# A hybrid decoder step: 64-token states in place of a 128-token product level, and the heads' tails split over two TensorE visits

## The chip, the core and the metric

The kernel runs on one core of a Trainium2 chip. The metric is the device time of one execution in microseconds (us); lower is better. The kernel before takes 1199.65 us (median of 3 runs, 1199.41 to 1201.19). Differences of 0.2% (2.4 us) are about what a measurement can tell here.

## What is computed

Two layers over a prompt group (16 learned meta tokens and 256 prompt tokens) and a sample group (8 sequences of 8 tokens), 336 columns in all. Layer 0 is a gated linear recurrence (HGRN2) with 16 heads of 128 x 128 state; layer 1 is sliding-window attention. The change touches layer 0 alone:

```python
def hgrn_chunk(q, logf, k, v, s0):
    b = jnp.cumsum(logf, axis=1)
    diff = jnp.where(causal, b[:, :, None] - b[:, None, :], -jnp.inf)
    a = jnp.sum(q[:, :, None] * jnp.exp(diff) * k[:, None, :], axis=-1)
    o = einsum('bthk,bhkv->bthv', q * exp(b), s0) + einsum('btsh,bshv->bthv', a, v)
    s_new = exp(b_last)[..., None] * s0 + einsum('bshk,bshv->bhkv', k * exp(b_last[:, None] - b), v)
    return o, s_new
# h = x @ w_in, split in q, fx, i, g; f = lb + (1-lb)*sigmoid(fx); k = 1-f; v = i
# prompt: a chunk of 16, then four of 64, the state handed on; sample: 8 tokens on a given state
# o * rsqrt(mean(o*o) + eps) * norm_w * silu(g), then o @ w_out, residual and LayerNorm
```

## The kernel before

All projections run as three fp32r matmuls (high and low halves of x and of the weights) into one PSUM tile `pj` per 128 output columns, issued by `Stream.run`. A head of layer 0 has four such tiles in the order f, q, i, g: 192 matmuls of 336 columns, two of whose operands wait for weights that ScalarE (ACT) and VectorE (DVE) split into `whi` and `wlo` seven chunks (of four times three matmuls) ahead. One call of `Stream.step` follows every three matmuls, and this "tick" is the clock of all side work: generators are spawned, and each `yield n` puts off the rest by n ticks. The order of the instructions on every engine is thus written out when the kernel is built; at run time an engine waits only where its next instruction's operands are late.

The recurrence of a head is `head_chain`. It doubles blocks: 1, 2, 4, 8, 16, 32, 64 tokens, `update` scaling k and q at each level by the running products `total`. TensorE is visited first for the levels 1 to 8 (tile `lv_a`, 48 products of 32 x 32), then for the levels 16, 32, 64 and 128 (tile `lv_b`, with the products `kr` x `qp` of 145 and 17 columns as the level of 128), then the transposes of k and v (`pk`, `pv`). ScalarE and VectorE gather all scores of a head in `at` and copy V, K, Vs, Ks out of PSUM; GpSimd (POOL) spreads Vs over `vm`.

What follows, `head_tail`, is a generator that the next head's chain advances (`adv(h - 1)`): outputs `po` and the prompt's last state `psp`; then squares and the norm (`ss`, raised to -1/2 on POOL); the scaled output `osc`; its transposes `pt` and the sample states' products `pss`; the gated output `og`, its halves `oh`, `ol`, and the sample states, scaled in place in `s0` and sent out. So TensorE is visited three times per head: `lv_a` with po and psp of the head before; pt and pss of the head before; `lv_b` with pk and pv. After the last head `tail_alone` advances the tail. PSUM has 3 tiles for `pj`, 2 for the levels (`lv`) and 3 for everything else (`mm`, taken by `pm`). The output projection (`z`, `oh` x `w_out`) follows head 15 at once; its first three tiles run chunk by chunk together.

Of the kernel before, what the change touches and what calls it, by code (L numbers as in the profile page):

```python
# [226 lines left out]
def hybrid_trunk(tc, x_prompt, x_sample, state_hgrn, cache_k, cache_v, meta, w_in0, lb_logits, norm_w, w_out0,  # L227
# [7 lines left out]
    with es:  # L235
# [84 lines left out]
        for nm, w in (("f", 384), ("qp", 448), ("iT", 384), ("ks", 256), ("at", 3 * 272), ("a32", 96), ("sq0", 256),  # L320
                      ("sq1", 256), ("w64", 64)):
            one[nm] = hp1.tile([P, w], F32, tag=nm, name=nm)
            nc.gpsimd.memset(one[nm], 1.0 if nm == "w64" else 0.0)
# [79 lines left out]
        def head_state(h):  # L403
            if h not in hd:
                hd[h] = dict(one, sq=one[f"sq{h % 2}"])
            return hd[h]

        def epi_f(h):
            def epi(ps):
# [11 lines left out]
                s0 = hp.tile([P, 8, P], F32, tag="s0", name=f"s0_{h}")  # L421
                nc.sync.dma_start(s0, state_hgrn[0, :, h].rearrange("b k v -> k b v"))
                d["s0"] = s0
# [8 lines left out]

        stage_of = {}
# [18 lines left out]
        def epi_g(h):  # L452
            def epi(ps):
                d = head_state(h)
                sg = hp.tile([P, T], F32, tag="sg", name=f"sg{h}")
                nc.scalar.activation(sg, ps, AF.Sigmoid)
                d["sg"] = sg

                def chain():
# [35 lines left out]

        tails = {}

        def adv(h):
            if h in tails:
                stage_of[h] += 1  # L500
                next(tails[h], None)

        def tail_alone(h):
            for w in (5, 4, 4, 2, 1):
                adv(h)
                yield w

        def head_chain(h):
            d = head_state(h)
            stage_of[h] = 0  # L510
            kr, qp, a32, s0, sq = d["kr"], d["qp"], d["a32"], d["s0"], d["sq"]
# [53 lines left out]
            adv(h - 1)  # L565
            yield 1
# [18 lines left out]
            nc.vector.tensor_tensor(t128[:, 1:2], t128[:, 0:1], t16, op=ALU.mult)  # L585
            nc.vector.tensor_scalar(qp[:, 255:272], qq[1][:, 255:272], t128[:, 0:1], None, op0=ALU.mult)
# [8 lines left out]
            yield 2  # L595
            adv(h - 1)
            yield 3
# [3 lines left out]
            pb = lv.tile([P, 512], F32, tag="lv", name=f"lv{h}_b")  # L601
            level(pb, 0, 4, wide=False)
            for blk in range(2):
# [5 lines left out]
                for a in range(2):  # L609
# [4 lines left out]
            nc.tensor.matmul(pb[:, 306:451], kr[:, 0:128], qp[:, 127:272], start=True, stop=True,  # L614
                             skip_group_check=True)
            nc.tensor.matmul(pb[:, 288:305], kr[:, 128:256], qq[1][:, 255:272], start=True, stop=True,
                             skip_group_check=True)
            iT = d["iT"]
            pk = pm(f"pk{h}")
            for j in range(2):  # L620
                nc.tensor.transpose(pk[:, j * P:(j + 1) * P], ks[:, j * P:(j + 1) * P], ident)
# [8 lines left out]
            for a in range(2):  # L630
                nc.scalar.copy(at[64 * a:64 * a + 32, 0:2, 64 * a + 31:64 * a + 63],
                               pb[64 * a:64 * a + 32, 96:160].rearrange("p (b w) -> p b w", b=2))
            nc.scalar.copy(at[0:64, 0:2, 63:127], pb[0:64, 160:288].rearrange("p (b w) -> p b w", b=2))
            for blk in range(3):
                nc.vector.copy_predicated(
                    at[:, blk, 0:128].rearrange("p (j w) -> p j w", w=32),
                    mk[:, 480 + blk * 128:608 + blk * 128].rearrange("p (j w) -> p j w", w=32),
                    a32[:, blk * 32:blk * 32 + 32].unsqueeze(1).to_broadcast([P, 4, 32]))
            nc.scalar.copy(at[:, 1, 127:144], pb[:, 288:305])
            nc.scalar.copy(at[:, 0, 127:272], pb[:, 306:451])  # L640
            V = hp.tile([P, 3, P], F32, tag="V", name=f"V{h}")
            K = hp.tile([P, 2, P], F32, tag="K", name=f"K{h}")
# [14 lines left out]
            tails[h] = head_tail(h, at, V, K, Ks, vm, fs)  # L657
            if h == H - 1:
                yield 6
                yield from tail_alone(h)  # L660

        def head_tail(h, at, V, K, Ks, vm, fs):
            d = head_state(h)
            s0, sq = d["s0"], d["sq"]
            po = pm(f"po{h}")
            psp = pm(f"psp{h}")
            for s in range(2):
                for j in range(4):
# [3 lines left out]
            nc.tensor.matmul(po[0:16, 256:384], at[:, 0, 256:272], V[:, 0, :], start=False, stop=False,  # L672
                             skip_group_check=True, tile_position=(0, 0))
            nc.tensor.matmul(po[0:16, 256:384], at[:, 1, 128:144], V[:, 1, :], start=False, stop=False,
                             skip_group_check=True, tile_position=(0, 0))
            nc.tensor.matmul(po[:, 256:384], at[:, 2, 0:128], V[:, 2, :], start=False, stop=True,
                             skip_group_check=True)
            nc.tensor.matmul(po[:, 128:256], at[:, 0, 128:256], V[:, 0, :], start=True, stop=False,
                             skip_group_check=True)
            nc.tensor.matmul(po[:, 128:256], at[:, 1, 0:128], V[:, 1, :], start=False, stop=True,  # L680
                             skip_group_check=True)
            nc.tensor.matmul(po[:, 0:128], at[:, 0, 0:128], V[:, 0, :], start=True, stop=True, skip_group_check=True)
            nc.tensor.matmul(psp[:, 0:128], K[:, 0, :], V[:, 0, :], start=True, stop=False)
            nc.tensor.matmul(psp[:, 0:128], K[:, 1, :], V[:, 1, :], start=False, stop=False)
            nc.tensor.matmul(psp[:, 0:128], K2, V[:, 2, :], start=False, stop=True)
            yield
            nc.gpsimd.tensor_tensor(s0, s0, fs.unsqueeze(2).to_broadcast([P, 8, P]), op=ALU.mult)
            sp = hp1.tile([P, P], F32, tag="sp", name=f"sp{h}")
            nc.scalar.copy(sp, psp[:, 0:128])
            nc.sync.dma_start(st_p[0, 0, h], sp)  # L690
# [11 lines left out]
            pt = pm(f"pt{h}")  # L702
            for j in range(3):
                nc.tensor.transpose(pt[:, j * P:(j + 1) * P], osc[:, j, :], ident)
            pss = []
            for u in range(2):
                pss.append(pm(f"pss{h}_{u}"))
                nc.tensor.matmul(pss[u], Ks[:, u, :], vm[0:112, 4 * u:4 * u + 4, :].rearrange("p b v -> p (b v)"),
                                 start=True, stop=True)
# [3 lines left out]
            nc.vector.scalar_tensor_tensor(og[:, 0:288], pt[:, 0:288], nw[:, h:h + 1], sg[:, 0:288], op0=ALU.mult,  # L713
                                           op1=ALU.mult)
# [5 lines left out]
            for u in range(2):  # L720
                s0u = s0[:, 4 * u:4 * u + 4, :].rearrange("p b v -> p (b v)")
                nc.vector.tensor_tensor(s0u, s0u, pss[u], op=ALU.add)
            nc.sync.dma_start(st_s[0, :, h].rearrange("b k v -> k b v"), s0)
# [641 lines left out]
```

## Time and profile before

| what | us |
|---|---|
| median of the runs | 1199.65 |
| the profiled execution | 1203.74 |
| its span | 1201.9 |
| TensorE busy in it | 1181.7 |
| VectorE busy | 793.3 |
| ScalarE busy | 625.6 |
| GpSimd busy | 244.0 |

Matmuls are pipelined and their ends are modelled, so what an instruction costs TensorE is read from its start to the next start. A fp32 product is two matmul instructions in the trace (x2 for one product).

### The profile page before, as it was taken

How to read it: one execution, taken by the hardware profiler on the slowest of the kernel's cores; microseconds unless marked ns; L12 is line 12 of the kernel's file. 1: busy time of each engine (PE TensorE's matmuls, PEld its weight loads, DVE VectorE, ACT ScalarE, POOL GpSimd, SP SyncE). 2: the span in 40 equal slices, each digit the busy share in tenths (PEclk: the TensorE clock that was granted, in tenths of full speed). 3: DMA queues.
4: the chain of work that ended last, by engine and by line, in shares of the span. 5: the costliest groups of instructions: out<-in, count | busy, mean ns of one | idle time of the engine just before them, and what ended most of it. 6: DMA issues, size and time to landing. Idle time of an engine off the chain costs nothing. (4 is left out here: it accounts for less than half of the span.)

```text
span 1201.9 us, 26362 instructions
## 1 busy us (share of the span) xinstructions
PE 1181.7 (98%) x10131; PEld 1135.6 (94%) x10131; DVE 793.3 (66%) x2017; ACT 625.6 (52%) x1827; POOL 244.0 (20%) x349
## 2 busy tenths in 40 slices
PE   9999999999999999999999999999999999999995
PEld 7999999999999999999999999988888899998994
DVE  4765666555666555656558777678778767776675
ACT  4655555554555454545445446665656655553330
POOL 3022112222112122112134332000000112144420
PEclk9999999999999999999999999999999999999997
DMA  9545654455654555654555555634244345564532
GB/s 263 157 134 150 178 144 133 137 144 157 178 144 120 150 144 159 167 149 119 150 144 140 145 146 165 182 105 129 73 117 127 90 123 159 152 170 139 148 89 88
DMA packets 328462, 171.48 MB, mean 143 GB/s; under 512 B 19084, under 2 KB 325612, under 8 KB 328166
## 3 DMA queue, kind: packets, MB, share of 16 engines
q1 hardware_dynamic: 327792, 168.82, 50.3%
q8 instruction: 80, 1.31, 0.5%
q0 software_dynamic: 544, 0.97, 0.2%
q14 instruction: 46, 0.38, 0.1%
HBM read 156.97 MB, written 14.42 MB: 143 GB/s over the span
## 5 line engine op out<-in xcount | busy, mean ns | idle before, releaser
L212 PE MATMUL pj_q<-xh,wlo_q 128*128 128x336 f32 (+1 forms) x512 | 165.9, 324 | 0.0
L212 PE MATMUL pj_g<-xh,wlo_g 128*128 128x336 f32 (+1 forms) x512 | 162.9, 318 | 0.0
L213 PE MATMUL pj_g<-xl,whi_g 128*128 128x336 f32 (+1 forms) x512 | 160.6, 314 | 0.0
L214 PE MATMUL pj_g<-xh,whi_g 128*128 128x336 f32 (+1 forms) x512 | 160.6, 314 | 0.0
L213 PE MATMUL pj_q<-xl,whi_q 128*128 128x336 f32 (+1 forms) x512 | 160.5, 314 | 0.0
L214 PE MATMUL pj_q<-xh,whi_q 128*128 128x336 f32 (+1 forms) x512 | 160.3, 313 | 0.0
L212 PEld LDWEIGHTS pj_q<-xh,wlo_q 128*128 128x128 f32 x512 | 96.7, 189 | 5.8 <-issue 4.7
L212 PEld LDWEIGHTS pj_g<-xh,wlo_g 128*128 128x128 f32 x512 | 96.7, 189 | 2.2 <-issue 1.3
L213 PEld LDWEIGHTS pj_g<-xl,whi_g 128*128 128x128 f32 x512 | 96.8, 189 | 0.8
L213 PEld LDWEIGHTS pj_q<-xl,whi_q 128*128 128x128 f32 x512 | 96.7, 189 | 0.5
L214 PEld LDWEIGHTS pj_g<-xh,whi_g 128*128 128x128 f32 x512 | 96.5, 189 | 0.0
L214 PEld LDWEIGHTS pj_q<-xh,whi_q 128*128 128x128 f32 x512 | 96.5, 189 | 0.0
L169 DVE TENSOR_TENSOR wlo_g<-raw_g,whi_g 128x512 fp32r<-128x512 f32 x128 | 90.4, 743 | 0.6 <-ACT whi_g L158 0.6
L169 DVE TENSOR_TENSOR wlo_q<-raw_q,whi_q 128x512 fp32r<-128x512 f32 x128 | 86.2, 684 | 3.9 <-ACT whi_q L158 3.9
L212 PE MATMUL pj_f<-xh,wlo_f 128*128 128x336 f32 x256 | 83.6, 326 | 0.0
L213 PE MATMUL pj_f<-xl,whi_f 128*128 128x336 f32 x256 | 81.5, 318 | 0.0
L212 PE MATMUL pj_i<-xh,wlo_i 128*128 128x336 f32 x256 | 81.4, 318 | 0.0
L214 PE MATMUL pj_f<-xh,whi_f 128*128 128x336 f32 x256 | 81.4, 318 | 0.0
L214 PE MATMUL pj_z<-oh,whi_z 128*128 128x336 f32 x256 | 81.1, 317 | 0.0
L212 PE MATMUL pj_z<-oh,wlo_z 128*128 128x336 f32 x256 | 81.1, 317 | 0.0
L213 PE MATMUL pj_z<-ol,whi_z 128*128 128x336 f32 x256 | 81.0, 316 | 0.0
L212 PE MATMUL pj_y<-ph,wlo_y 128*128 128x320 f32 x256 | 81.0, 316 | 0.0
(410 smaller groups left out, 3219.4 us busy)
## 6 DMA issues: line engine op xcount, KB each, us to landing
raw_g<-in_hgrn_w_in_dram SPq DMA_DIRECT2D x32, 512.0 KB
raw_z<-in_hgrn_w_out_dram SPq DMA_DIRECT2D x32, 512.0 KB
raw_q<-in_swa_w_in_dram SPq DMA_DIRECT2D x32, 512.0 KB
raw_g<-in_swa_w_in_dram SPq DMA_DIRECT2D x32, 512.0 KB
raw_y<-in_swa_w_out_dram SPq DMA_DIRECT2D x32, 512.0 KB
raw_f<-in_hgrn_w_in_dram SPq DMA_DIRECT2D x30, 512.0 KB
raw_q<-in_hgrn_w_in_dram SPq DMA_DIRECT2D x30, 512.0 KB
raw_i<-in_hgrn_w_in_dram SPq DMA_DIRECT2D x30, 512.0 KB
```

Source lines behind the costliest of these rows:

```text
L169: e.nc.vector.tensor_tensor(lo, t.pop(("raw", kc)), hi.bitcast(F32), op=ALU.subtract)
L212: nc.tensor.matmul(ps, lo[:, kk, :], xh, start=first, stop=False)
L213: nc.tensor.matmul(ps, hi[:, kk, :], xl, start=False, stop=False)
L214: nc.tensor.matmul(ps, hi[:, kk, :], xh, start=False, stop=last)
```

## The change

- The level of 128 is gone: no products of 145 and 17 columns, no scaled copy `ks`. `kr` is now scaled only to the end of each 128-token block and is transposed itself. `at` holds 132 columns per block, for scores within 128 tokens and one column's shift.
- `psp` holds three separate products (block 0, block 1, the 16 tokens behind). From them S[0] (state behind token 127), S[1] (behind token 255) and the last state `sp` are built by a copy and two scalar-tensor operations on VectorE. Queries scaled to a block's start stand in a new tile `qi` (two of them, by turns); they meet S[0] and S[1] in `po`.
- The tail's stages stand in another order and are advanced by the next two heads: psp and pss in the next head's `lv_a` visit, po inside its `lv_b` visit, the norm and `osc` behind that, pt in the `lv_a` visit of the head after that (into the PSUM tile of the next head's `lv_b`), then og.
- Sample states are scaled out of place into `ns`; `s0` is loaded at the end of a head's g tile and not of its f tile; V and K have one buffer and not two. `og` takes three operations for the first 288 columns in place of one.
- After head 15 the rest of head 14's tail and head 15's own run in one sequence.

```diff
-                      ("sq1", 256), ("w64", 64)):
+                      ("sq1", 256), ("qi0", 177), ("qi1", 177), ("w64", 64)):
...
             for li in range(4):
                 level(pa, 96 * li, li)
             adv(h - 1)
+            adv(h - 2)
             yield 1
...
             yield 3
-            adv(h - 1)
+            adv(h - 2)
             update(kk[1], qq[1], 32, tot[32], 256, kk[2], qq[2])
+            nc.scalar.copy(qi[:, 144:161], qq[1][:, 255:272])
...
-            update(kk[2], qq[2], 64, t64, 256, kr, qp, nq=True)
-            nc.scalar.copy(qp[:, 127:191], qq[2][:, 127:191])
-            ks = d["ks"]
-            nc.scalar.activation(ks[:, 0:128], kr[:, 0:128], AF.Copy, scale=t128[:, 1:2])
-            nc.scalar.activation(ks[:, 128:256], kr[:, 128:256], AF.Copy, scale=t16)
+            k64 = kk[2]
+            nc.vector.tensor_tensor(halves(kr, 0, 64, 256), halves(k64, 0, 64, 256),
+                                    t64.rearrange("p (b two) -> p b two", two=2)[:, :, 1:2].to_broadcast([P, 2, 64]),
+                                    op=ALU.mult)
+            nc.scalar.copy(halves(kr, 0, 64, 256, True), halves(k64, 0, 64, 256, True))
+            nc.vector.tensor_scalar(qi[:, 64:128], qq[2][:, 191:255], t64[:, 2:3], None, op0=ALU.mult)
+            nc.scalar.copy(qi[:, 0:64], qq[2][:, 127:191])
...
-            nc.tensor.matmul(pb[:, 306:451], kr[:, 0:128], qp[:, 127:272], start=True, stop=True,
-                             skip_group_check=True)
-            nc.tensor.matmul(pb[:, 288:305], kr[:, 128:256], qq[1][:, 255:272], start=True, stop=True,
-                             skip_group_check=True)
+            adv(h - 1)
...
-            if h == H - 1:
-                yield 6
-                yield from tail_alone(h)
+            if h < H - 1:
+                yield 2
+                adv(h - 1)
+                yield 2
+                adv(h - 1)
+                return
+            yield 1
+            adv(h - 1)
+            yield 2
+            adv(h - 1)
+            yield 1
+            adv(h)
+            adv(h - 1)
...
+        def head_tail(h, at, V, K, Ks, vm, fs, t16, t128):
+            psp = pm(f"psp{h}")
+            for j, (a, v) in enumerate(((K[:, 0, :], V[:, 0, :]), (K[:, 1, :], V[:, 1, :]), (K2, V[:, 2, :]))):
+                nc.tensor.matmul(psp[:, j * P:(j + 1) * P], a, v, start=True, stop=True, skip_group_check=True)
+...
+            yield
+            nc.scalar.copy(S[:, 0, :], psp[:, 0:P])
+            nc.vector.scalar_tensor_tensor(S[:, 1, :], S[:, 0, :], t128[:, 0:1], psp[:, P:2 * P], op0=ALU.mult,
+                                           op1=ALU.add)
+            nc.vector.scalar_tensor_tensor(sp, S[:, 1, :], t16, psp[:, 2 * P:3 * P], op0=ALU.mult, op1=ALU.add)
+            nc.gpsimd.tensor_tensor(ns, s0, fs.unsqueeze(2).to_broadcast([P, 8, P]), op=ALU.mult)
+            yield
...
+            yield
...
-            nc.tensor.matmul(po[0:16, 256:384], at[:, 0, 256:272], V[:, 0, :], start=False, stop=False,
-            nc.tensor.matmul(po[0:16, 256:384], at[:, 1, 128:144], V[:, 1, :], start=False, stop=False,
-            nc.tensor.matmul(po[:, 256:384], at[:, 2, 0:128], V[:, 2, :], start=False, stop=True,
-            nc.tensor.matmul(po[:, 128:256], at[:, 0, 128:256], V[:, 0, :], start=True, stop=False,
+            for j, c in ((0, 145), (1, 128)):
+                nc.tensor.matmul(po[32 * j:32 * j + 32, 256:384], qi[:, c:c + 32], S[:, 1, :], start=False,
+                                 stop=False, tile_position=(0, 32 * j), skip_group_check=True)
+            for j in (2, 3, 0, 1):
+                nc.tensor.matmul(po[32 * j:32 * j + 32, 256:384], at[:, 2, 32 * j:32 * j + 32], V[:, 2, :],
+                                 start=False, stop=True, tile_position=(0, 32 * j), skip_group_check=True)
+            nc.tensor.matmul(po[:, 128:256], qi[:, 0:128], S[:, 0, :], start=False, stop=True, skip_group_check=True)
...
+            pt = hd[h + 1]["pb"] if h < H - 1 else pm(f"pt{h}")
```

On TensorE, the `lv_a` visit of head 7 in the kernel before, from its last level on (`po_4274` and `psp_4275` belong to head 6):

```order
L521 MATMUL lv_a<-qx_174,kx_172 32x32 x12
L670 MATMUL po_4274<-s_6_3517,sq_158 32x128 x8
L672 MATMUL po_4274<-V_3955,at 16x128
L674 MATMUL po_4274<-V_3955,at 16x128
L676 MATMUL po_4274<-V_3955,at 128x128
L678 MATMUL po_4274<-V_3955,at 128x128
L680 MATMUL po_4274<-V_3955,at 128x128
L682 MATMUL po_4274<-V_3955,at 128x128
L683 MATMUL psp_4275<-V_3955,K_3956 128x128
L684 MATMUL psp_4275<-V_3955,K_3956 128x128
L685 MATMUL psp_4275<-V_3955,K_176 128x128
```

The same visit in the changed kernel (`osc_3976` is head 5's):

```order
L516 MATMUL lv_a<-qx_176,kx_174 32x32 x12
L680 MATMUL psp_4263<-V_3937,K_3938 128x128 x2
L680 MATMUL psp_4263<-V_3937,K_178 128x128
L684 MATMUL pss_0_4267<-vm_3947,Ks_3943 128x512
L684 MATMUL pss_1_4269<-vm_3947,Ks_3943 128x512
L734 MATMUL lv_b<-ident,osc_3976 128x128 x3
```

All of po has left this visit, and what was a visit of its own (pss, and the transposes of osc) has come in.

On TensorE, the `lv_b` visit of head 7 in the kernel before:

```order
L521 MATMUL lv_b<-qx_174,kx_172 32x32 x9
L606 MATMUL lv_b<-qx_166,kx_164 32x32 x2
L611 MATMUL lv_b<-qx_170,kx_168 32x64 x2
L606 MATMUL lv_b<-qx_166,kx_164 32x32 x2
L611 MATMUL lv_b<-qx_170,kx_168 32x64 x2
L614 MATMUL lv_b<-qp,kr_4026 128x145
L616 MATMUL lv_b<-qx_166,kr_4026 128x17
L621 MATMUL pk_4439<-ident,ks 128x128
L622 MATMUL pk_4439<-ident,kS 112x128
```

The same visit in the changed kernel, from the last level product on (`po_4406` is head 6's):

```order
L607 MATMUL lv_b<-qx_172,kx_170 32x64 x2
L707 MATMUL po_4406<-s_6_3866,sq_156 32x128 x8
L710 MATMUL po_4406<-S_4289,qi_160 32x128 x2
L713 MATMUL po_4406<-V_3937,at 32x128 x4
L715 MATMUL po_4406<-V_3937,at 128x128
L717 MATMUL po_4406<-S_4289,qi_160 128x128
L718 MATMUL po_4406<-V_3937,at 128x128
L614 MATMUL pk_4424<-ident,kr_4017 128x128
L615 MATMUL pk_4424<-ident,kS 112x128
```

The two wide level products are gone, and po stands between the levels and the transposes; of its products six are now 32 columns wide, besides the eight of before.

On GpSimd, behind the last head's `lv_b` visit in the kernel before (`ss_8392` and `s_14` are head 14's, the rest head 15's):

```order
L687 TENSOR_TENSOR s_14_7597<-s_14_7597,fs_7759 128x1024
L696 TENSOR_TENSOR ss_8392<-ss_8392,mhalf 128x3
L653 TENSOR_TENSOR vm_8555<-Vs_8550,cst 112x512 x2
L687 TENSOR_TENSOR s_15_8107<-s_15_8107,fs_8271 128x1024
L696 TENSOR_TENSOR ss_8631<-ss_8631,mhalf 128x3
```

The same place in the changed kernel (`ss_8553` is head 14's):

```order
L695 TENSOR_TENSOR ns_8383<-s_14_7954,fs_7755 128x1024
L645 TENSOR_TENSOR vm_8546<-Vs_8541,cst 112x512 x2
L725 TENSOR_TENSOR ss_8553<-ss_8553,mhalf 128x3
L695 TENSOR_TENSOR ns_8598<-s_15_8465,fs_8268 128x1024
L725 TENSOR_TENSOR ss_8663<-ss_8663,mhalf 128x3
```

Head 14's norm stands behind head 15's `vm` now. TensorE comes to the products that need vm and to the transposes of head 14's osc, which need this norm, 15 matmuls of z after the visit.

## Rows read from the trace of the kernel before

**Rows 1.** Busy time by stretch, heads 0 to 15: PE PEld DVE ACT POOL, PEclk, DMA.

```profile
50.00:620.00 570.00, 570.00 (x5916) 555.71 (x5915) 344.73 (x987) 298.21 (x1015) 117.46 (x156) 1.00 0.54 148
```

**Rows 2.** Timeline, TensorE, a head's lv_a visit: start, us, engine, line, out<-in.

```profile
331.89 0.40 PE L521 MATMUL lv_a<-qp,kr 128*32 128x32 f32 x24
...
332.94 0.64 PE L670 MATMUL po<-s,sq 128*32 128x128 f32 x16
333.38 0.38 PE L672 MATMUL po<-V,at 128*16 128x128 f32 x2
333.60 0.38 PE L674 MATMUL po<-V,at 128*16 128x128 f32 x2
333.91 0.49 PE L676 MATMUL po<-V,at 128*128 128x128 f32 x2
334.23 0.39 PE L678 MATMUL po<-V,at 128*128 128x128 f32 x2
334.45 0.39 PE L680 MATMUL po<-V,at 128*128 128x128 f32 x2
...
335.49 0.40 PE L212 MATMUL pj_g<-xh,wlo_g 128*128 128x336 f32 x1
```

**Rows 3.** Timeline, TensorE, the same head's middle visit.

```profile
339.71 0.49 PE L704 MATMUL pt<-ident,osc 128*128 128x128 f32 x3
...
340.52 0.32 PE L212 MATMUL pj_g<-xh,wlo_g 128*128 128x336 f32 x1
...
340.98 0.31 PE L212 MATMUL pj_g<-xh,wlo_g 128*128 128x336 f32 x1
```

**Rows 4.** Timeline, TensorE, the same head's lv_b visit.

```profile
342.92 0.34 PE L521 MATMUL lv_b<-qx,kx 128*32 128x32 f32 x17
...
343.58 0.51 PE L614 MATMUL lv_b<-qp,kr 128*128 128x145 f32 x2
343.93 0.29 PE L616 MATMUL lv_b<-qx,kr 128*128 128x17 f32 x2
344.07 0.31 PE L621 MATMUL pk<-ident,ks 128*128 128x128 f32 x1
...
344.99 0.38 PE L212 MATMUL pj_f<-xh,wlo_f 128*128 128x336 f32 x1
```

**Rows 5.** Timeline, VectorE, between these visits; in brackets the idle time before.

```profile
337.14 0.17 DVE L695 TENSOR_SCALAR ss<-ss 128x3 f32<-128x3 f32 x1 [2.33 <-ACT junk L694]
...
340.93 0.28 DVE L479 TENSOR_TENSOR kr<-kx,tot 128x128 f32<-128x128 f32 x1
...
341.87 0.51 DVE L713 SCALAR_TENSOR_TENSOR og<-pt,tv,sg 128x288 f32<-128x288 f32 x1
342.30 0.26 DVE L715 SCALAR_TENSOR_TENSOR og<-pt,tv,sg 128x48 f32<-128x48 f32 x1
...
343.52 1.28 DVE L722 TENSOR_TENSOR s<-s,pss 128x512 f32<-128x512 f32 x2
```

**Rows 6.** Timeline, ScalarE, GpSimd and VectorE behind the last head's lv_b visit.

```profile
600.82 0.50 ACT L643 COPY V<-pv 128x384 f32<-128x384 f32 x1
...
601.61 0.25 ACT L648 COPY Vs<-pv 112x128 f32<-112x128 f32 x1
...
601.93 2.49 POOL L653 TENSOR_TENSOR vm<-Vs,cst 112x512 fp32r<-112x512 f32 x2 [9.89 <-ACT Vs L648]
...
606.65 1.22 POOL L696 TENSOR_TENSOR ss<-ss,mhalf 128x3 f32<-128x3 f32 x1 [0.37 <-DVE ss L695]
...
607.91 0.56 DVE L699 TENSOR_TENSOR osc<-po,ss 128x384 f32<-128x384 f32 x1 [0.74 <-POOL ss L696]
```

**Rows 7.** A wait of TensorE later on, and busy time by stretch behind it.

```profile
1088.12 0.55 PE L1205 MATMUL yt<-ident,z 128*128 128x128 f32 x3 [2.88 <-DVE z L1195]
...
1088.00:1091.00 3.00, 2.88 (x15) 2.89 (x16) 2.56 (x10) 2.00 (x4) 1.28 (x2) 0.69 0.57 165
1091.00:1094.00 3.00, 3.00 (x18) 2.99 (x17) 1.83 (x5) 1.40 (x3) 2.31 (x3) 0.74 0.63 182
```

More of the change, by code (lines that the diff above doesn't have):

```diff
@@ L404, in head_state @@
             if h not in hd:
-                hd[h] = dict(one, sq=one[f"sq{h % 2}"])
+                hd[h] = dict(one, sq=one[f"sq{h % 2}"], qi=one[f"qi{h % 2}"])
             return hd[h]
@@ L457, in epi @@
                 d["sg"] = sg
+                s0 = hp.tile([P, 8, P], F32, tag="s0", name=f"s0_{h}")
+                nc.sync.dma_start(s0, state_hgrn[0, :, h].rearrange("b k v -> k b v"))
+                d["s0"] = s0
                 def chain():
@@ L620, in head_chain @@
             for j in range(2):
-                nc.tensor.transpose(pk[:, j * P:(j + 1) * P], ks[:, j * P:(j + 1) * P], ident)
+                nc.tensor.transpose(pk[:, j * P:(j + 1) * P], kr[:, j * P:(j + 1) * P], ident)
                 nc.tensor.transpose(pk[0:112, (j + 2) * P:(j + 3) * P], kS[:, j, :].bitcast(F32), ident)
@@ new lines, in head_chain @@
+            yield 1
[5 more added lines that the diff above has]
+            adv(h - 1)
+            yield 1
+            adv(h)
+            adv(h - 1)
+            yield 1
+            adv(h)
+            yield 3
+            adv(h)
+            for w in (4, 3, 2, 1):
+                yield w
+                adv(h)
+        def head_tail(h, at, V, K, Ks, vm, fs, t16, t128):
+            d = head_state(h)
+            s0, sq, qi = d["s0"], d["sq"], d["qi"]
+            psp = pm(f"psp{h}")
+            for j, (a, v) in enumerate(((K[:, 0, :], V[:, 0, :]), (K[:, 1, :], V[:, 1, :]), (K2, V[:, 2, :]))):
+                nc.tensor.matmul(psp[:, j * P:(j + 1) * P], a, v, start=True, stop=True, skip_group_check=True)
+            pss = []
+            for u in range(2):
+                pss.append(pm(f"pss{h}_{u}"))
+                nc.tensor.matmul(pss[u], Ks[:, u, :], vm[0:112, 4 * u:4 * u + 4, :].rearrange("p b v -> p (b v)"),
+                                 start=True, stop=True)
+            yield
+            S = hp1.tile([P, 2, P], F32, tag="S", name=f"S{h}")
+            nc.scalar.copy(S[:, 0, :], psp[:, 0:P])
+            nc.vector.scalar_tensor_tensor(S[:, 1, :], S[:, 0, :], t128[:, 0:1], psp[:, P:2 * P], op0=ALU.mult,
+                                           op1=ALU.add)
+            sp = hp1.tile([P, P], F32, tag="sp", name=f"sp{h}")
+            nc.vector.scalar_tensor_tensor(sp, S[:, 1, :], t16, psp[:, 2 * P:3 * P], op0=ALU.mult, op1=ALU.add)
+            nc.sync.dma_start(st_p[0, 0, h], sp)
+            ns = hp1.tile([P, 8, P], F32, tag="ns", name=f"ns{h}")
+            nc.gpsimd.tensor_tensor(ns, s0, fs.unsqueeze(2).to_broadcast([P, 8, P]), op=ALU.mult)
+            yield
+            for u in range(2):
+                nu = ns[:, 4 * u:4 * u + 4, :].rearrange("p b v -> p (b v)")
+                nc.vector.tensor_tensor(nu, nu, pss[u], op=ALU.add)
+            nc.sync.dma_start(st_s[0, :, h].rearrange("b k v -> k b v"), ns)
+            yield
@@ L665, in head_tail @@
             po = pm(f"po{h}")
-            psp = pm(f"psp{h}")
             for s in range(2):
@@ L701, in head_tail @@
             yield
-            pt = pm(f"pt{h}")
+            pt = hd[h + 1]["pb"] if h < H - 1 else pm(f"pt{h}")
             for j in range(3):
                 nc.tensor.transpose(pt[:, j * P:(j + 1) * P], osc[:, j, :], ident)
[L705 to L709, printed above, removed]
             yield
@@ L719, in head_tail @@
             split(oh[h], ol[h], og)
[L720 to L723, printed above, removed]
         tiles = {}
```

56 lines of the change are left out of this document (15 added, 41 removed).

## The prediction

> **What bounds the kernel now.** I read the busy time by stretch first, then the TensorE timeline of one head, then the timelines of the engines that feed it. Over the stretch of the sixteen heads TensorE is busy in 570.0 of 570 us at a granted clock of 1.00, that is 2.4 GHz, while VectorE has 345 us and ScalarE 298 us [rows 1]. Busy time of pipelined matmuls alone proves little, but in the timeline the starts of a head follow one another without a wait: in none of the three visits does a row name a releaser [rows 2 to 4]. So in this layer a matmul that goes away is time that goes away, and other engines count only where TensorE comes to wait for them. The three visits are read from start to start: 3.60 us for the first (331.89 to 335.49), 0.81 for the second (339.71 to 340.52), and the levels of the third up to the transposes 1.15 (342.92 to 344.07) [rows 2 to 4]. The layer behind it does not change, and I take nothing there.
>
> **Products that go, per head.** The level of 128 costs 0.35 us for 145 columns (343.58 to 343.93) and 0.14 for 17 (343.93 to 344.07) [rows 4]. In po, the two products with 16 columns of weights cost 0.22 (333.38 to 333.60) and 0.31, and the full product behind them 0.32 (333.91 to 334.23), while the plain full product after that costs 0.22 [rows 2]. I read 0.09 of the 0.31 and 0.10 of the 0.32 as the turn from narrow to full weights, which the new po has too, so these count 0.22 each, 0.66 in all. The 145 columns by the same scale would be 0.22 x 145/128 = 0.25; the 0.10 above that is again such a turn, from the levels to full weights, and it moves to the first visit, where psp now follows the levels. Removed: 0.25 + 0.14 + 0.66 = 1.05 us.
>
> **Products that come.** Six products with 32 columns of weights (two with qi, four with at). The same shape stands in the trace: eight of them, dealt out over four column groups, take 0.44 (332.94 to 333.38), 0.055 each [rows 2]. Six are 0.33. The bounds: if they all slipped in beside others, 0; if each cost as much as a 16-column product whose successor is in the same group, 0.22, then 1.32. I take 0.33, since shape, groups and operands are those of the row. The qi pair lies in groups 0 and 1 alone, but the at products begin with groups 2 and 3, so neighbours still differ.
>
> The Trainium skill (TensorE: Matmul & The Clock Gate, section Measured speedup vs the span model) has three column tiles together only 2.38 times as fast as one by one, and says that weight loads overlap only between row groups. The trace does not agree so far: eight in 0.44 against eight full ones in 1.8 is four times. By the rule six would cost 0.22 x 6/2.38 = 0.56, an estimate, and the gain be 3.7 us less.
>
> **Products that move.** The three psp and the two pss, the three transposes of osc, one full product with at for block 1 and one for block 0 are the same shapes as before, one at product is replaced by one of qi x S[0] of equal size: nothing but place. What is gained at the edges is that one visit less is entered and left. The second visit shows no gap at its edges, so I put 0.05 there, between 0 and 0.15. Per head: -1.05 + 0.33 - 0.05 = -0.77 us; sixteen heads: **-12.3 us**.
>
> **What covers the rest.** Between the visits VectorE gets more to do before kr is finished, and TensorE now needs more of it: pk waits for kr and, for its PSUM tile, for the first addition of the sample states. Before, kr ended at 340.93 + 0.28 = 341.21. From this goes the idle 2.33 us before ss, because the squares are now taken behind the third visit, and osc, 0.56 [rows 5, 6]. To it come og, ol and the state additions, which stood behind it from 341.87 to 344.80, that is 2.93; S[1], sp and og's two extra operations, at no more than the 0.26 of a small scalar-tensor operation each [rows 5]: kr at 341.21 - 2.33 - 0.56 + 2.93 + 4 x 0.26 = 342.3. TensorE enters the third visit at 342.92, less the second visit's 0.81, less what the first loses: 3.60 becomes 1.05 for the levels, 0.2 for the turn, 0.66 for psp and 0.81, together 2.7. That is 341.2. It reaches pk only after levels with turn (0.66) and po (0.44 + 0.33 + 0.66), 2.1 later, at 343.3. Slack 1.0 us, so I cost it at nothing; every us by which I am wrong beyond it costs 15 us (third rival). POOL's scaling of s0 no longer waits for po, since it writes to ns; it is early. ScalarE loses three instructions per head, and its copies to at now wait until po has been read, half way through the visit: behind them are the V and K copies, which wait for the visit's end anyway. SP sends the state output earlier; behind its wait on ns are only weight loads, four buffers deep. s0 is loaded three tiles, 144 matmuls, later than before, and used a head later; only head 15's po needs it some 11 us after its issue (sum below). I take it to land in time; each us that it is late costs one, once.
>
> **The last head.** Here nothing separates the visits. After the last lv_b visit come 15 matmuls of z (three take 0.46 [rows 3], so 2.3 us), then psp and pss of head 15 and the transposes of head 14's osc. Count from the visit's start: 2.1 to pk and 0.92 for pk and pv (344.07 to 344.99 [rows 4]), 3.0. TensorE is at psp at 3.0 + 2.3 = 5.3, and through psp and the first pss at 6.4. ScalarE starts V at 3.25, just after pv; Vs follows V by 0.79, vm on POOL starts 0.32 after Vs and takes 2.49 [rows 6]. The norm of head 14 is queued behind vm on POOL and takes 1.22, then osc 0.56 [rows 6]: 3.25 + 0.79 + 0.32 + 2.49 + 1.22 + 0.04 + 0.56 = 8.7, with the semaphore 8.8. TensorE waits **2.4 us**, between 0 (if vm and the norm are quicker by as much) and 5 (if ScalarE is behind by that). In the kernel before, 22 matmuls stood between the visit and the tail, and the norm was not behind another head's vm. A wait has an aftermath: behind the 2.88 us wait the granted clock was 0.69 and 0.74 over 6 us, so it had fallen to 1.2 GHz, a loss of 6 x 0.285 = 1.7 us [rows 7]. 2.4 is near to 2.88, so I add **1.7**; it is 0 if the clock stays. Two more, small visits: 0.1. Head 15's po then meets S[1] (VectorE has it 1 us after osc, TensorE is 2.3 us of z away), and its pt comes 27 matmuls of z (4.1 us) after po, of which norm and osc need 0.37 + 1.22 + 0.56 = 2.2 [rows 6] and leave 1.9 to three squares: no more waits.
>
> **Sum.** -12.3 + 2.4 + 1.7 + 0.1 = -8.1 us. The profiled execution took 1203.74 (its span 1201.9), so it would become 1195.6. It stood 4.1 above the median of the runs; from that median, 1199.65, the forecast is **1191.5 us**, 0.7% faster.
>
> **Rivals.**
> - *No wait at the last head.* The POOL norm comes before TensorE needs it, or the wait is so short that the clock stays. For it: POOL is otherwise idle there, and V may be copied earlier than I reckon. Against: vm and the norm alone are 3.7 us on one engine, and TensorE gives them 3.4 after the visit (6.4 less 3.0). Without wait and clock loss: 1187.4.
> - *Column groups do not overlap as in the row*, because the six hang on few groups. If they ran two at a time, at 0.22/2 = 0.11 each, six would take 0.66, 0.33 more per head, 5.3 in all: 1196.8. Against it stand the eight equal products at 0.055. The rule of the Trainium skill above points this way.
> - *VectorE becomes the bound at pk* (the other sign). For it: VectorE is in order, and osc now waits on it for POOL's norm, with weight splits and f behind; og, ol and the state additions are all ahead of kr. If kr came 3 us later than reckoned, 2.0 us would be lost at fifteen visits, 30 us: 1221. It decides from 8.1/15 = 0.54 us of wait per visit on, that is from kr 1.5 us later. Against: VectorE is busy 60% of this stretch [rows 1], and the operations at an upper price.
> - *The visits cost more than their products*: merging three into two saves more at the edges (up to 0.15 per head, 1.6 more in all) and the 145 columns are wholly saved (0.10 per head, 1.6): 1188.3 with the wait, 1184.2 without.
>
> **How the numbers follow.** Forecast with its neighbours (1189 to 1194): 0.5. No wait at the last head, or larger edges: 0.27. Column groups or a longer wait at the last head (1194 to 1198): 0.13. VectorE at pk: 0.06, nearly all slower. Small losses of both kinds that add up to nothing (within 0.2%, 2.4 us, about what a measurement can tell): 0.04. Faster 0.9, same 0.04, slower 0.06. The range from 1184 to 1197 holds the forecast, the first, second and fourth rival, and leaves out the third.
>
> **What would show it.** Right: a head's period shorter by about 0.8 us, two visits per head; the six narrow products in about 0.33 us; no L614/L616 of 145 and 17 columns; one wait of TensorE of 1 to 4 us near the end of layer 0, released by osc, with a lower clock after it; layer 1 as long as before. Wrong: waits of TensorE at pk, released by VectorE, in each head; a narrow product at 0.1 us or more; or a wait for s0 at the last po.

## The result, and the profile after

The changed kernel takes 1191.52 us (median of 6 runs, 1189.07 to 1193.61); the kernel before, run beside it, 1200.5 (6 runs, 1199.41 to 1204.94). The ratio is 0.9918, with a 95% interval of 0.9904 to 0.9932: 0.7 to 1.0% faster. The forecast was 1191.5. The profiled execution of after took 1193.07 (span 1191.3), that of before 1203.74.

Busy time by stretch, kernel after, where [rows 1] stood before; PE PEld DVE ACT POOL, PEclk, DMA share, GB/s:

```profile
50.00:620.00 570.00, 568.44 (x6007) 555.17 (x6006) 349.65 (x1033) 286.22 (x977) 113.74 (x166) 1.00 0.53 150
```

TensorE still bounds the heads, at full clock; 1.56 us of it is idle now, and that is one wait. Timeline of TensorE, kernel after, an `lv_a` visit, which answers to [rows 2] and the middle visit of [rows 3]; start, us, engine, line, out<-in:

```profile
328.64 0.40 PE L516 MATMUL lv_a<-qp,kr 128*32 128x32 f32 x24
...
329.68 0.94 PE L680 MATMUL psp<-V,K 128*128 128x128 f32 x6
330.37 0.71 PE L684 MATMUL pss<-vm,Ks 112*128 112x512 f32 x2
330.92 0.49 PE L734 MATMUL lv_b<-ident,osc 128*128 128x128 f32 x3
331.17 0.40 PE L212 MATMUL pj_g<-xh,wlo_g 128*128 128x336 f32 x1
```

The same head's `lv_b` visit, which answers to [rows 4]:

```profile
337.79 0.34 PE L516 MATMUL lv_b<-qx,kx 128*32 128x32 f32 x17
...
338.25 0.30 PE L707 MATMUL po<-s,sq 128*32 128x128 f32 x2
...
338.71 0.28 PE L713 MATMUL po<-V,at 128*32 128x128 f32 x2
338.75 0.30 PE L710 MATMUL po<-S,qi 128*32 128x128 f32 x2
...
338.97 0.41 PE L713 MATMUL po<-V,at 128*32 128x128 f32 x4
339.32 0.49 PE L715 MATMUL po<-V,at 128*128 128x128 f32 x2
339.64 0.39 PE L717 MATMUL po<-S,qi 128*128 128x128 f32 x2
...
340.09 0.27 PE L614 MATMUL pk<-ident,kr 128*128 128x128 f32 x1
...
340.97 0.39 PE L212 MATMUL pj_f<-xh,wlo_f 128*128 128x336 f32 x1
```

Read from start to start: the first visit takes 2.53 us (forecast 2.7), the second 3.18 (forecast 2.1 + 0.92, 3.0). No row in them names a releaser. From the first of the eight sq products to the first full product of po it is 1.07, where the forecast had 0.77. Of these 0.30, 0.20 are the turn from narrow to full weights, which the forecast had counted with the levels (337.79 to 338.25 is 0.46 here, 342.92 to 343.58 was 0.66 in [rows 4]); the other 0.1 is what the six narrow products cost beyond their price. From head to head the start of `lv_a` moves on by 35.59 us, where it was 36.28 before: 0.69 less, forecast 0.77. The visits shown differ by 0.77 (6.48 and 5.71), but the first visit of the kernel before takes 3.49 to 3.60 from head to head, and the one of [rows 2] is among the longest; over thirteen heads the visits come to 6.41 and 5.73 on average, with 29.88 of projections between them in both kernels.

VectorE in kernel after, where [rows 5] stood:

```profile
337.75 0.28 DVE L585 TENSOR_TENSOR kr<-kx,tot 128x128 f32<-128x128 f32 x1
```

kr is ready at 338.03 and read at 340.09: 2.06 us of slack, where I had reckoned 1.0.

Behind the last head's `lv_b` visit (which begins at 586.89) in kernel after, timelines of TensorE, ScalarE, GpSimd and VectorE; they answer to [rows 6], and brackets give the idle time and what ended it:

```profile
592.45 0.83 PE L680 MATMUL psp<-V,K 128*128 128x128 f32 x6
593.04 0.48 PE L684 MATMUL pss<-vm,Ks 112*128 112x512 f32 x1
595.07 0.47 PE L684 MATMUL pss<-vm,Ks 112*128 112x512 f32 x1 [1.56 <-DVE osc L728]
...
590.22 0.48 ACT L635 COPY V<-pv 128x384 f32<-128x384 f32 x1
...
591.34 2.04 POOL L645 TENSOR_TENSOR vm<-Vs,cst 112x512 fp32r<-112x512 f32 x2 [15.02 <-ACT Vs L640]
593.49 0.85 POOL L725 TENSOR_TENSOR ss<-ss,mhalf 128x3 f32<-128x3 f32 x1
...
592.77 0.63 DVE L724 TENSOR_SCALAR ss<-ss 128x3 f32<-128x3 f32 x1 [1.55 <-ACT junk L723]
594.37 0.56 DVE L728 TENSOR_TENSOR osc<-po,ss 128x384 f32<-128x384 f32 x1 [0.96 <-POOL ss L725]
```

The wait that was forecast is there, at that place and released by osc, but 1.56 us long and not 2.4. The second product of pss is the one that stands, though it does not read osc; by the kernel's text it takes one of the three `mm` tiles, and osc is what reads head 14's po out of one. Ahead of the norm, vm ends at 593.38 on GpSimd and the norm's input at 593.40 on VectorE, so this trace does not tell which of the two held the norm. Busy time by stretch around it, the granted clock third from the right:

```profile
593.00:596.00 3.00, 1.44 (x10) 1.08 (x9) 2.00 (x5) 0.51 (x2) 1.23 (x2) 1.00 0.95 260
596.00:599.00 3.00, 3.00 (x43) 2.71 (x41) 2.46 (x6) 1.52 (x3) 1.71 (x1) 1.00 0.02 6
```

The clock did not fall, unlike in [rows 7].

**A yardstick for the comparisons.** The whole time mixes the change with two ends that vary. I therefore use the stretch from the start of the first `lv_a` visit to the first product of layer 1 (`pj_k`): all heads and the output projection. It is 669.7 us before (50.44 to 720.1) and 660.7 after (52.58 to 713.3): 8.9 less.

### The profile page after: what moved, and what is told of

The parts are those of the page before. It is cut to its first block, busy times and chain, and to the rows that moved or that the text cites. A ratio compares the mean times of both kernels' runs of the same rounds, so it can differ in the third digit from the quotient of the medians.

```text
span 1191.3 us, 26295 instructions
## 1 busy us (share of the span) xinstructions
PE 1170.4 (98%) x10163; PEld 1125.5 (94%) x10163; DVE 792.3 (67%) x2049; ACT 609.9 (51%) x1779; POOL 236.8 (20%) x350
## 4 chain that ended last, share of the span: by engine, by line
PE 92%; issue 3%; DVE 2%; DMA 1%; ACT 1%; POOL 1%; SPq 0%; POOLq 0%; DVEq 0%; ACTq 0%
PE pj_q L212 7%; PE pj_g L212 7%; PE pj_g L213 7%; PE pj_g L214 6%; PE pj_q L213 6%; PE pj_q L214 6%; PE pj_f L212 4%; PE pj_i L212 3%; PE pj_i L214 3%; PE pj_i L213 3%; PE pj_f L214 3%; PE pj_f L213 3%; PE pj_z L214 3%; PE pj_z L213 3%; PE pj_z L212 3%
## 5 line engine op out<-in xcount | busy, mean ns | idle before, releaser
L213 PE MATMUL pj_i<-xl,whi_i 128*128 128x336 f32 x256 | 80.9, 316 | 0.0
```

The costliest lines, as they stand in the source:

```text
L213: nc.tensor.matmul(ps, hi[:, kk, :], xl, start=False, stop=False)
```

## The experiments

Times are medians, ratios are to the kernel before with their 95% interval, and "stretch" is the yardstick above.

**The kernel after once more.**

> The changed kernel itself once more, beside the edits of it. Theory (the heads bring the whole gain, the two ends of the trace vary by themselves): time 1191.5 us within 0.2%; from the first lv_a visit to the last lv_b visit again 534.3 us within 0.3, while the start of the first lv_a visit (52.58 us in the first profile against 50.44 of before) and the wait for yt in layer 1 (1.23 us against 2.88) may come out at other values. Rival (the change itself makes the start 2.1 us later and the end 3.9 us shorter): the first visit again at 52.6 within 0.3, the wait again at 1.2 within 0.3.

1191.33 us, 0.9913 (0.9898 to 0.9928). Stretch 660.8 (49.66 to 710.4), and from the first `lv_a` visit to the last `lv_b` 534.2. The ends differ. Start of the program, stretch 10 to 20 us, first kernel after, then this repetition (the clock is third from the right):

```profile
10.00:20.00 10.00, 9.07 (x35) 7.30 (x35) 3.60 (x6) 4.48 (x9) 2.50 (x6) 0.57 1.10 287
```

```profile
10.00:20.00 10.00, 9.93 (x54) 7.91 (x53) 4.00 (x7) 4.52 (x10) 3.47 (x7) 0.92 1.15 284
```

In layer 1, TensorE's wait for `yt` in the first profile of after and in the repetition:

```profile
1079.71 0.55 PE L1227 MATMUL yt<-ident,z 128*128 128x128 f32 x3 [1.23 <-DVE z L1217]
```

```profile
1077.84 0.55 PE L1227 MATMUL yt<-ident,z 128*128 128x128 f32 x3 [2.79 <-DVE z L1217]
```

The same program starts its heads 2.9 us earlier and waits 1.6 us longer at the end. Theory right: the later start and the shorter end in the first profile of after are not the change's doing.

**The kernel before once more.**

> The kernel before once more, for its trace. Theory (the profiled execution of before was a long one, 1203.7 against a median of 1200.5, and what it had too much lies in the ends of the trace): from the first lv_a visit to the first product of layer 1 again 669.7 us within 0.5; the rest (start, wait for yt, clock at the end) comes out 1 to 3 us shorter. Rival (the heads vary too): that stretch differs by more than 1 us.

One time, 1202.62. Stretch 669.7 (52.40 to 722.1), the same as in the first profile. Its start had the low clock (0.57 from 10 to 20 us), its wait for `yt` was 1.1 us and not 2.9. The theory holds: the heads repeat within 0.1 us, and the ends differ, the start 2.0 us longer, the part from `pj_y` (layer 1's output projection) on 3.1 us shorter (137.3 against 140.4).

**The narrow products: one product in place of four.** A column group is 32 columns of the array; a product with 32 columns of weights stands on one of the four, a full product on all.

```diff
-            for j in (2, 3, 0, 1):
-                nc.tensor.matmul(po[32 * j:32 * j + 32, 256:384], at[:, 2, 32 * j:32 * j + 32], V[:, 2, :], ...)
+            nc.tensor.matmul(po[:, 256:384], at[:, 2, 0:128], V[:, 2, :], start=False, stop=True, ...)
```

> After, with the four narrow products of at and V on the third block (32 columns each, four column groups) replaced by one product over the whole array. Theory from the trace of after (the six narrow products behind the eight of s0 and sq take 0.09 us each and not the 0.055 forecast, and the array's turn of 0.1 us is there either way): 0.13 us a head less, -2.0 us, 1189.4. Rival (the forecast's price, 4 x 0.055 = 0.22 against one product of 0.22): no change, within 0.5 us of after.

1192.65 us, 0.9928 (0.9914 to 0.9943); stretch 660.6. My theory fell: there is no gain. TensorE in this kernel, the same part of a `lv_b` visit:

```profile
337.43 0.30 PE L707 MATMUL po<-s,sq 128*32 128x128 f32 x2
...
337.94 0.41 PE L710 MATMUL po<-S,qi 128*32 128x128 f32 x4
338.28 0.49 PE L712 MATMUL po<-V,at 128*128 128x128 f32 x2
```

From the first sq product to the first full product it is now 0.85, 0.22 less than the 1.07 of after, and one full product at 0.22 has come in. So the four cost 0.22 together, 0.055 each, as forecast. Then the excess must sit with the pair of qi, which lies on column groups 0 and 1 alone. That gave the next two runs.

**Two narrow products from the loaded groups, two from the others.** Without the products of qi and S on the third block (a part of the outputs is left out):

```diff
-            for j, c in ((0, 145), (1, 128)):
-                nc.tensor.matmul(po[32 * j:32 * j + 32, 256:384], qi[:, c:c + 32], S[:, 1, :], ...)
```

> After, without the two narrow products of qi and S on the third block, which stand on column groups 0 and 1 alone (that part of the output is left out). Theory (narrow products on different column groups run side by side, each taking 0.22 us as the full one does, so that the longest group decides: groups 0 and 1 have two of sq, one of qi and one of at, 4 x 0.22; groups 2 and 3 have 3 x 0.22): the longest group goes from four to three, -0.22 x 16 = -3.5 us, 1187.9. Rival (each narrow product costs the same quarter, 0.055, as the prediction had it): -0.11 x 16 = -1.8 us, 1189.6.

1187.92 us, 0.9894 (0.9881 to 0.9908); stretch 657.1, 3.6 below after. TensorE in this kernel:

```profile
334.12 0.30 PE L707 MATMUL po<-s,sq 128*32 128x128 f32 x2
...
334.58 0.46 PE L710 MATMUL po<-V,at 128*32 128x128 f32 x8
334.97 0.49 PE L712 MATMUL po<-V,at 128*128 128x128 f32 x2
```

0.85 in place of 1.07: two products of 32 columns were worth 0.22, a full product's time. The counterpart leaves out two of the at products instead:

```diff
-            for j in (2, 3, 0, 1):
+            for j in (0, 1):
                 nc.tensor.matmul(po[32 * j:32 * j + 32, 256:384], at[:, 2, 32 * j:32 * j + 32], V[:, 2, :], ...)
```

> After, without the two narrow products of at and V on column groups 2 and 3 (that part of the output is left out); groups 0 and 1 keep theirs. It is the counterpart of the run without qi, which took two narrow products from groups 0 and 1 and came out at 1187.9. Theory (the longest column group decides; it still has four products): no change, 1191.4 within 1 us, and 0.61 us from the first of the narrow products to the first full one as in after. Rival (every narrow product costs a share): -0.11 to -0.2 a head, -1.8 to -3.5 us, 1189.6 to 1187.9.

1190.23 us, 0.9909 (0.9893 to 0.9925); stretch 660.5, 0.2 below after and not 1.8 to 3.5. TensorE in this kernel:

```profile
335.88 0.30 PE L707 MATMUL po<-s,sq 128*32 128x128 f32 x2
...
336.38 0.41 PE L710 MATMUL po<-S,qi 128*32 128x128 f32 x4
336.60 0.41 PE L713 MATMUL po<-V,at 128*32 128x128 f32 x4
336.94 0.49 PE L715 MATMUL po<-V,at 128*128 128x128 f32 x2
```

1.06, as in after. Two products of the same shape cost 0.22 or nothing, by the group that they stand on. Products on different column groups run side by side, each lasting as long as a full one, and the longest group sets the time: two of sq, one of qi and one of at, 4 x 0.22 = 0.88; with the turn to full weights behind them, 0.19, this is the 1.07, and with one product less on that group the 0.85. The six that came in thus cost 2 x 0.22 = 0.44, not 0.33. Another reading of these runs would be that each set of operands (s and sq, S and qi, V and at) takes rounds of its own. The rows speak against it: in after the at products of groups 2 and 3 begin at 338.71, in one round with those of qi at 338.75 though issued behind them, and the at products of groups 0 and 1 only at 338.97. Here, where groups 2 and 3 have none, the at products begin at 336.60, 0.22 behind qi.

**The wide level products alone, taken out of the kernel before.** It leaves out the 145 and 17 columns and the two copies into `at` that read them (part of the scores).

```diff
-            nc.tensor.matmul(pb[:, 306:451], kr[:, 0:128], qp[:, 127:272], ...)
-            nc.tensor.matmul(pb[:, 288:305], kr[:, 128:256], qq[1][:, 255:272], ...)
...
-            nc.scalar.copy(at[:, 1, 127:144], pb[:, 288:305])
-            nc.scalar.copy(at[:, 0, 127:272], pb[:, 306:451])
```

> The kernel before, without its 145-column and its 17-column product in the lv_b visit and without the two copies into at that read them (that part of the scores is left out of the output). It measures one of the prediction's terms by itself. Theory (the prediction's terms: 0.25 for the 145 columns and 0.14 for the 17, a head): -0.39 x 16 = -6.2 us, 1194.6 against 1200.9. Rival (the wide product also pays the turn of the array and its edges, 0.49 a head or more): -7.8 us or more, 1193.0.

1196.61 us, 0.9964 (0.9953 to 0.9976); stretch 664.0, 5.7 below before, or 0.36 a head. By the stretch the theory's 6.2 looks right; the visits say otherwise. TensorE behind the levels in two neighbouring heads of this kernel:

```profile
412.04 0.33 PE L617 MATMUL pk<-ident,ks 128*128 128x128 f32 x1
412.20 0.27 PE L618 MATMUL pk<-ident,kS 128*112 128x128 f32 x1
...
448.22 0.27 PE L618 MATMUL pk<-ident,kS 128*112 128x128 f32 x1
448.48 0.55 PE L621 MATMUL pv<-ident,iT 128*128 128x128 f32 x3
```

The visit shrinks from 2.07 to 1.60 in every second head: the two products cost 0.46 to 0.47 there, since without them the turn of the array to full weights costs pk little (0.16 to the next start). That is nearly the rival's 0.49, the whole step from 343.58 to 344.07 in [rows 4]. In the other heads 0.2 comes back: from the last pk transpose to pv it is 0.26 and not 0.11, a stop without a releaser in the trace. Its cause is open. In the changed kernel this step is 0.10 in the visit shown, so the 0.47 is the nearer price there; that is an argument, not a measurement.

**A visit of its own.**

```diff
             adv(h - 1)
-            adv(h - 2)
             yield 1
+            adv(h - 2)
```

> After, with the three transposes of the output of head h-2 (pt) taken out of the lv_a visit and given one tick later, a visit of their own of each head, as the kernel before had a third visit. Theory (a visit costs what its products take and one turn of the array): 0.05 us a head, +0.8 us, 1192.3. Rival (each visit has a price of its own of 0.15 us or more): +2.4 us or more, 1193.9.

1191.96 us, 0.992 (0.9907 to 0.9933); stretch 661.0, 0.3 above after. TensorE in this kernel, end of the `lv_a` visit (which began at 292.76) and the new visit:

```profile
295.03 0.32 PE L212 MATMUL pj_g<-xh,wlo_g 128*128 128x336 f32 x1
...
295.49 0.49 PE L734 MATMUL lv_b<-ident,osc 128*128 128x128 f32 x3
295.74 0.40 PE L212 MATMUL pj_g<-xh,wlo_g 128*128 128x336 f32 x1
```

2.27 + 0.25 = 2.52, against 2.53 in one visit. This visit of three transposes costs its products and nothing measurable besides: the 0.05 per head that I had credited to the merged visit is at most 0.02.

**VectorE's slack at pk.** Four, then ten additions of 128x256 ahead of kr:

```diff
+            for _ in range(4):    # 10 in the second kernel
+                nc.vector.tensor_tensor(scr, cst[:, 0:256], cst[:, 152:408], op=ALU.add)
             nc.vector.tensor_tensor(halves(kr, 0, 64, 256), ...
```

> After, with four more VectorE additions of 128x256 (about 0.35 us each, 1.4 us together) ahead of the multiplication that makes kr in every head; kr is transposed into pk 2.0 us after it is made in the trace of after. Theory (the slack at pk is 2.0 us and nothing else on VectorE is near its limit): no change, within 1 us of after (1191.4). Rival (the prediction's slack of 1.0 us): late by 0.4 us x 15 heads = +6 us, 1197.

> After, with ten such additions ahead of kr (about 3.5 us). Theory (slack of 2.0 us at pk): late by 1.5 us x 15 heads = +22 us, 1214, with PE waiting at the transposes of kr. Rival (the slack of 1.0 us): 2.5 x 15 = +37 us, 1229. Second rival (VectorE's time is not on the path at all): no change.

Four take 1.80 us and the heads keep their 35.59: kr comes 1.7 later and TensorE does not wait at pk, so the slack exceeds 1.7. The time is still 1195.09, 0.9957 (0.9942 to 0.9972), 3.7 above after, which no theory had. Part of it stands at the last head. TensorE there in this kernel, and the busy time by stretch:

```profile
593.72 0.77 PE L687 MATMUL pss<-vm,Ks 112*128 112x512 f32 x1 [2.14 <-DVE osc L731]
```

```profile
594.00:596.00 2.00, 2.00 (x8) 1.82 (x8) 1.61 (x7) 0.00 (x0) 0.00 (x0) 0.50 0.16 48
596.00:598.00 2.00, 2.00 (x11) 2.00 (x11) 1.46 (x2) 1.52 (x3) 1.81 (x1) 0.72 0.00 0
```

The wait is 2.14 in place of 1.56, and now the clock falls, to 1.2 GHz (0.50) and back: from psp to po it is 8.08 us and not 5.67, 2.4 more for a wait that is 0.6 longer. That is the forecast's aftermath. The stretch is 663.1, those 2.4 more; the remaining 1.3 of the median are not in this execution, which was the shortest of its four runs.

Ten additions give 1240.68, 1.0334 (1.032 to 1.0348), further off than every theory: an addition takes 0.46 from start to start and not 0.35, kr comes 4.5 later, and TensorE waits 16 times at pk, 36.6 in all. From the visit's start to pk it is 4.88 and no longer 2.30; 4.5 less these 2.6 is a slack of 1.9, near the 2.06 read. The rest is largely the clock. Busy time by stretch around two such waits, each 2.42 long:

```profile
248.00:251.00 3.00, 3.00 (x17) 3.00 (x16) 1.99 (x8) 2.01 (x10) 0.33 (x1) 0.62 0.33 81
...
287.00:290.00 3.00, 2.76 (x21) 2.79 (x22) 2.19 (x9) 1.21 (x6) 0.00 (x0) 1.00 0.13 35
```

Behind the first, which ended at 247.43, the clock fell; behind the second, at 287.24, it did not. Of the fourteen waits of 2.37 to 2.42 us it fell behind five, every third one, and these periods are 39.7 us long where their neighbours have 38.2 (it also fell behind the first head's wait of 2.11). So the length of a wait does not decide by itself. The last head says the same: in this kernel, with ten additions, the product of pss waits as long as with four, and the clock stays:

```profile
642.49 0.47 PE L687 MATMUL pss<-vm,Ks 112*128 112x512 f32 x1 [2.13 <-DVE osc L731]
```

```profile
642.00:645.00 3.00, 2.52 (x17) 2.48 (x18) 2.42 (x9) 0.54 (x2) 0.47 (x1) 1.00 0.51 151
```

And so do the waits for `yt` in layer 1: the clock stayed at 1.00 behind 2.79 us in the repetition of after, and fell (to 0.54 over the next 3 us) behind 1.95 us in the run without the qi products.

**The wait at the last head taken away.**

```diff
             yield 2
             adv(h - 1)
-            yield 1
+            yield 7
             adv(h)
             adv(h - 1)
```

> After, with the last head's own tail started six more ticks later, so that TensorE has other products to do while VectorE waits for the vm products and the norm of head 14 on GpSimd. Theory (the 1.56 us of idle TensorE ahead of the pss products of head 15 is all that this place costs, and no clock falls there): the wait goes and the time is 1.6 us below that of after, 1189.9. Rival (the last head's chain has no work to lie behind, so the wait comes back at the tail's later steps): within 0.5 us of after, with a wait of 1 us or more at a later product of head 15.

1191.52 us, 0.9916 (0.9902 to 0.993): no gain in time. Yet the wait is gone, and nothing came in its place. TensorE at the last head in this kernel:

```profile
592.91 0.83 PE L680 MATMUL psp<-V,K 128*128 128x128 f32 x6
593.49 0.70 PE L684 MATMUL pss<-vm,Ks 112*128 112x512 f32 x2
594.04 0.49 PE L734 MATMUL lv_b<-ident,osc 128*128 128x128 f32 x3
```

The stretch is 658.9, 1.8 below after: the theory's 1.6. The profiled execution gave it back in layer 1, where TensorE waits, and the clock behind it:

```profile
1077.57 0.82 PE L1227 MATMUL yt<-ident,z 128*128 128x128 f32 x3 [3.09 <-DVE z L1217]
```

```profile
1077.00:1080.00 3.00, 2.43 (x10) 2.44 (x11) 2.28 (x9) 1.59 (x3) 1.73 (x2) 0.62 0.65 175
```

VectorE stood there for the load of `yg` (1 MB), issued behind the weights' loads. So the next run split that load.

**yg in two transfers.**

```diff
-            nc.sync.dma_start(Y["g"], ln_g[1:2, :].to_broadcast([P, D]))
+            nc.sync.dma_start(Y["g"][:, 0:256], ln_g[1:2, 0:256].to_broadcast([P, 256]))
+            nc.sync.dma_start(Y["g"][:, 256:D], ln_g[1:2, 256:D].to_broadcast([P, D - 256]))
```

> After, with the load of yg (1 MB) in layer 1 split in two transfers, of which the first (256 columns) is all that the first two multiplications read. Theory (PE's wait for yt, 1.2 us in one execution of after and 2.8 in another, is that transfer's time): the wait goes and the time falls by 1 to 3 us, 1189.4. Rival (the small transfer lands no sooner, since it queues behind the weights' loads that are under way): wait and time as in after, within 0.5 us.

1191.98 us, 0.9919 (0.9904 to 0.9934): no gain. TensorE's wait for `yt` became 0.54 us in this execution. From the issue of the load to VectorE's first multiplication with it 6.2 us pass here, and 7.0 in the next run, which has the same edit; with the whole load it was 6.9 in after, 8.5 in its repetition and 8.8 with the late tail. The small transfer lands sooner by little, if at all. Nearer to the rival.

**Both.**

> After, with both: the last head's tail six ticks later and yg in two transfers. Theory (the tail alone took 1.8 us off the stretch up to layer 1 and the wait for yt gave it back at the end; without that wait both gains stay): 1.8 us below the run with yg in two alone, 1187.6. Rival (something else near the end keeps the time): no faster than the run with yg in two alone.

1188.74 us (5 runs, 1188.41 to 1188.98), 0.9893 (0.9875 to 0.991). It beats both kernels: every run of it is below every run of the two single edits. Stretch 658.9; the wait for `yt` 1.25, and no clock loss behind it. The theory gave 1.8 below the split alone; measured were 3.2. Between the two profiled executions (3.3 apart) the stretch makes 1.8 and an earlier start (50.43 against 52.10) 1.7; why the other runs of this kernel are lower by as much stays open. The wait for `yt` is that of after (1.23), so the 1.8 of the late tail are shown, a share of the split load is not.

## Why the prediction was right

**The bound.** Right: TensorE bounds the heads. Products taken out of the longest column group, or of all four, showed up as time in the stretch; between 50 and 620 us no wait of TensorE but the one at the last head stands in the trace, and the additions measured VectorE's slack at pk.

**The heads: -12.3 forecast, -10.5 measured** (8.9 off the stretch, and the 1.56 of the wait that it contains, so small losses at the last head are in it too). The step "Six are 0.33" was mis-sized. Six equal products were priced at an average over eight that filled all four column groups evenly. These six do not: groups 0 and 1 get two each. They cost 0.44; 16 x 0.11 = 1.8 is this step's miss. The speedup in the Trainium skill (TensorE: Matmul & The Clock Gate, section Measured speedup vs the span model) gave 0.56, an estimate (0.22 x 6/2.38 is nearer 0.55); the truth lay half way. What the runs with two products less show is a count per group, not one speedup for all. The second rival, which spoke of "few groups", had the right cause and too high a price, 0.66. Two smaller steps offset each other, if the visit of every second head is taken for the wide level products: they were worth 0.47 and not 0.39, because the turn that I had left standing went with them, and the merged visit gave 0.01 and not 0.05. With the 0.66 for the old po, which no run measured by itself: -0.47 - 0.66 + 0.44 - 0.01 = -0.70; measured -0.69. Of these terms the 0.44 is shown; the others are an account that fits, and with the 0.36 a head by which the stretch without the wide products fell it would be -0.59. Sixteen times 0.69 is 11.0; the 0.5 that the 10.5 lacks stands mainly behind the start of the last head and is not traced.

**The last head: +4.1 forecast, +1.56 measured.** Place and releaser were right, and so was the chain from the norm on; whether vm ahead of it or its input set its start is not shown, since both end within 0.02 us. TensorE reached psp 5.56 behind the visit's start (5.3 forecast) and V began at 3.33 (3.25). But vm took 2.04 and not 2.49, the norm 0.85 and not 1.22: the 0.8 by which the wait was shorter. The 1.7 for the clock was 0. In all seven profiled executions with the wait of 1.5 to 1.6 the clock of that part stayed at 1.00; with 2.14 it fell once and with 2.13 it stayed once. The step "2.4 is near to 2.88, so I add 1.7" took the length of the wait for the cause, and the runs show that it does not suffice: what else decides stays open.

**The cover at pk.** Right that it costs nothing, with more room than reckoned: kr came 0.24 behind the visit's start, not 1.1, and pk 2.30, not 2.1.

**s0.** It landed at 597.29, when GpSimd's product with it began, 0.8 us ahead of po at 598.12: in time, barely.

**The sum.** Two errors of opposite sign, +1.8 in the heads and -2.5 at the last head, left -8.9 in the stretch against -8.1. The base also moved: 1199.65 of three runs became 1200.5 to 1201.4 in the later ones, so that by the ratio the gain is 8.2 to 11.5. To meet 1191.5 within 0.1 us is luck; the sign and the size within 1 us are not.

## What to carry to other kernels

Price narrow products by the column group that holds most of them, not by an average: fill the groups evenly, and further ones are free until a group becomes the longest. Where TensorE is the bound, the whole of a program's time can still hide a gain of 2 us behind a start and an end that vary; compare the stretch that the edit touches, in two executions of each kernel. A wait of 2 us can cost another 1.8 by the clock in one execution and nothing in another, so price that loss as a chance, and read several traces before calling it absent.

## What was not expected of the hardware

- Products on different column groups overlap fully and uneven groups do not share: two of the same shape cost 0.22 us on the longest group and less than 0.02 on a shorter one.
- Entering and leaving one more visit, of three 128x128 transposes between the projection's matmuls, costs 0.01 us (2.27 + 0.25 against 2.53, with as little in the stretch: 0.3 us in sixteen heads).
- The same wait of about 2.4 us lowered the clock five times in fourteen, at every third head, and left it at 2.4 GHz the other times; 1.95 us lowered it where 2.79 did not. The Trainium skill (TensorE: Matmul & The Clock Gate, section Part 1: The HAM clock gate) says that the block which sets the clock watches TensorE in a free-running way, which does not start anew with a kernel. By that equal waits could end differently, and one in three at equal distances agrees with it; no run here isolates it.
- The start of the program runs at a granted clock of 0.57 to 0.59 between 10 and 20 us in five of the fourteen profiled executions, of either kernel, and at 0.92 or 1.00 in the others. In the five the first `lv_a` visit begins at 52.1 to 52.6 us, in the others at 49.7 to 50.5, and everything behind it is moved with it.
